# Time mixing of a decoder trunk: projections with features on partitions, plain float32 stationary weights, masks applied while a bank is emptied

## The chip, the core and the metric

The kernel runs on one core of one Trainium2 chip. The metric is the device time of the whole program in microseconds (us). A core has five instruction queues that matter here: TensorE (PE, with weight loads in a row of their own, PEld), VectorE (DVE), ScalarE (ACT), GpSimd (POOL) and SyncE (SP), which issues the transfers. Each engine executes its own instructions in order and waits for others on semaphores.

## The reference, cut to what matters

A two-layer decoder trunk with T = 256 tokens and D = 1024 features: a SwiGLU feed-forward, RWKV-7 time mixing, a second feed-forward, one shared K/V, and then a layer of feed-forward, windowed attention, feed-forward. All in float32. The part at issue is the time mixing of the first layer:

```python
xr, xw, xk, xv, xa, xg = [x + xx * mu[i] for i in range(6)]
r = xr @ w_rkv[0]
k = xk @ w_rkv[1]
v = xv @ w_rkv[2]
w = -jax.nn.softplus(-(w0 + jnp.tanh(xw @ w1) @ w2)) - 0.5
decay = jnp.exp(-jnp.exp(w.astype(f32)))
a = jax.nn.sigmoid(a0 + (xa @ a1) @ a2)
g = jax.nn.sigmoid(xg @ g1) @ g2
kk = heads(k * k_k)
kk = kk / jnp.maximum(jnp.linalg.norm(kk, axis=-1, keepdims=True), 1e-12)
k = k * (1.0 + (a - 1.0) * k_a)
b_h = kk * a_h
def step(S, inp):                        # over 256 tokens, 16 heads of 64
    sa = jnp.einsum('bhij,bhj->bhi', S, -kk_t)
    S = S * w_t + sa[..., None] * b_t + v_t[..., None] * k_t
    return S, jnp.einsum('bhij,bhj->bhi', S, r_t)
bonus = jnp.sum(r_h * k_h * r_k, axis=-1, keepdims=True) * v_h
return ((groupnorm(y) + bonus) * g) @ w_o
```

## The kernel before, in words

Weights of the feed-forwards, of keys, of receptance and of w_o are split into a high part (rounded to fp32r, on ACT, L145) and a low part (the difference, on DVE, L151, or in two halves on POOL, L149), and a product is three passes, high by high, high by low, low by high (mm3, L169, L173, L174). A list of numbers per stage (PK, PR, PWO and others) says which low parts POOL computes. Weights come in chunks of 512 KB through four buffers named wr, issued in order by SP.

The time mixing lies between the first and the second feed-forward. It uses the chunked form of the recurrence, with four chunks of 64 tokens. Tokens are in two halves of 128 (i = 0, 1). First come the shift difference xx and the mixes (L435). The low-rank projections of decay, rate and gate (tm_lora, L508, plain float32) and their second factors (L552) follow. Keys are projected per token half, tokens on partitions (tok_half), and so is the receptance for both halves (tok_both). With tokens on partitions, `keys` squares on ACT, sums per head on DVE (L562), raises to the power -1/2 on POOL (L564) and scales (L565); `decays` makes the running sum of the decay with a triangular matrix Lc (L576) and two exponentials (L581, L582), and takes 24 rows out of the result with 24 small transfers (L585); `elem` multiplies (L591 to L597, on POOL and DVE). Because the recurrence needs features on partitions, `flip` turns each of eight [128, 1024] tiles with eight PE transposes into two banks (L632) and copies the banks (L635) into the tiles AR (decayed receptance and minus the keys' direction) and BK (the other factors).

From AR and BK the diagonal blocks of 32x32 are formed (L663), copied out (L669) and inverted by a solver of 31 steps on DVE, two instructions per step (L696, L698). The values' projection (L498, plain float32, both halves) runs on PE beside the solver. Then come g_pass, three passes of 32 matmuls over 64 partitions (L721), whose banks ACT empties (L731, L784), masks on DVE (L729, eight of 128x1024), the product with the inverse (L813, L822), the two state steps (u_step L833, x_step L842), the biases and gates of the group norm (L770, L774, L780 to L782), the state S (L879, L882), the outputs (L863), the group norm (L909 to L922), and the projection with w_o.

The order of the instructions on each engine is made at build time by a scheduler that plays a timeline; the code's order is its input, and `mark` and `plan` add dependences for the splits. PSUM has six banks named bk and two named bt.

## Time and profile before

| what | before |
|---|---|
| time, median of 3 runs | 1136.38 us (1135.64 to 1136.39) |
| time of the profiled execution | 1136.9 us |
| span of its profile | 1135.1 us |
| granted TensorE clock, mean | 0.97 |
| PE busy | 1081.9 us, 95% |
| DVE busy | 667.5 us, 59% |
| ACT busy | 528.6 us, 47% |
| POOL busy | 153.4 us, 14% |

The time-mixing stage begins where PE ends the first feed-forward, shortly after 203 us, and the second feed-forward begins near 453 us. Outside this stretch PE is busy nearly throughout and at full clock. A number behind "x" is a count of instructions; PEclk is the granted TensorE clock, where 1.00 is full and 0.50 half; "<-" names what ended an engine's idle time. A float32 matmul stands in the profile as two records.

### The profile page before, as it was taken

To read this page: it belongs to the slowest core of one execution; us is meant where nothing else is said; L and a number is where in the kernel's file an instruction comes from. 1 tells how busy PE (TensorE), PEld (TensorE's weight loads), DVE (VectorE), ACT (ScalarE), POOL (GpSimd) and SP (SyncE) were. 2 spreads that over 40 slices of the span, in tenths; PEclk is the share of its full clock that TensorE was granted. 3 is DMA by queue.
4 is the path that set the end of the run, shared out by engine and by line. 5 is a ranking of instruction groups with operands and counts; after the bars stand their busy time and mean duration, and the time that the engine had idled before them with its cause. 6 is when DMAs were issued, how large, how long until landed. Compare 5 with 4: busy or idle time off the path is not lost.

```text
span 1135.1 us, 18594 instructions
## 1 busy us (share of the span) xinstructions
PE 1081.9 (95%) x7704; PEld 962.4 (85%) x7704; DVE 667.5 (59%) x843; ACT 528.6 (47%) x781; POOL 153.4 (14%) x113
## 2 busy tenths in 40 slices
...
GB/s 265 231 175 294 199 175 149 112 19 127 135 149 38 2 59 140 213 221 198 230 187 161 118 150 222 186 242 187 183 131 167 130 54 188 223 198 192 186 130 38
DMA packets 53651, 181.61 MB, mean 160 GB/s; under 512 B 9152, under 2 KB 9408, under 8 KB 53440
## 3 DMA queue, kind: packets, MB, share of 16 engines
...
q10 hardware_dynamic: 288, 0.52, 0.1%
q14 instruction: 23, 0.19, 0.1%
...
## 4 chain that ended last, share of the span: by engine, by line
PE 77%; DVE 7%; issue 5%; POOL 4%; ACT 3%; DMA 2%; SPq 1%; POOLq 0%; DVEq 0%; ACTq 0%
PE bk L173 22%; PE bk L174 22%; PE bk L169 22%; POOL W L149 4%; PE bk L498 2%; DVE W L151 1%; PE bk L721 1%; DVE xi L435 1%; ACT W L145 1%; PE bt L721 1%; DMA wr<-in_w_in_dram 1%; PE bk L1051 1%; SPq L585 1%; PE bk L833 1%; PE bt L250 1%
## 5 line engine op out<-in xcount | busy, mean ns | idle before, releaser
L151 DVE TENSOR_TENSOR W<-wr,W 128x1024 fp32r<-128x1024 f32 x274 | 347.0, 1273 | 296.2 <-ACT W L145 296.0
L145 ACT CAST W<-wr 128x1024 fp32r<-128x1024 f32 x308 | 320.3, 1048 | 396.0 <-PE bk L174 266.4
L169 PE MATMUL bk<-xth,W 128*128 128x256 f32 x1184 | 335.4, 283 | 0.0
L174 PE MATMUL bk<-xth,W 128*128 128x256 f32 x1184 | 334.8, 283 | 0.0
L173 PE MATMUL bk<-xtl,W 128*128 128x256 f32 x1184 | 334.7, 283 | 0.0
L173 PEld LDWEIGHTS bk<-xtl,W 128*128 128x128 f32 x1184 | 226.6, 191 | 1.3
L169 PEld LDWEIGHTS bk<-xth,W 128*128 128x128 f32 x1184 | 226.2, 191 | 1.3
L174 PEld LDWEIGHTS bk<-xth,W 128*128 128x128 f32 x1184 | 226.4, 191 | 0.0
L149 POOL TENSOR_TENSOR W<-wr,W 128x512 fp32r<-128x512 f32 x68 | 109.6, 1637 | 335.1 <-ACT W L145 331.9
L173 PE MATMUL bk<-W,g2k 128*128 128x512 f32 x352 | 137.8, 391 | 0.0
L169 PE MATMUL bk<-W,g2k 128*128 128x512 f32 x352 | 137.2, 391 | 0.0
L174 PE MATMUL bk<-W,g2k 128*128 128x512 f32 x352 | 136.7, 390 | 0.0
L183 POOL TENSOR_TENSOR rs<-rs,mhalf 128x1 f32<-128x1 f32 x24 | 13.2, 552 | 604.1 <-DVE rs L180 603.9
L169 PE MATMUL bk<-W,xth 128*128 128x256 f32 (+1 forms) x288 | 89.5, 315 | 3.9 <-ACT xth L255 3.9
L174 PE MATMUL bk<-W,xtl 128*128 128x256 f32 (+1 forms) x288 | 89.1, 313 | 1.7 <-DVE xtl L256 1.6
L173 PE MATMUL bk<-W,xth 128*128 128x256 f32 (+1 forms) x288 | 88.9, 312 | 0.6 <-DVE W L151 0.5
L174 PEld LDWEIGHTS bk<-W,g2k 128*128 128x128 f32 x352 | 66.1, 188 | 14.1
L169 PEld LDWEIGHTS bk<-W,g2k 128*128 128x128 f32 x352 | 66.2, 188 | 13.1
L173 PEld LDWEIGHTS bk<-W,g2k 128*128 128x128 f32 x352 | 66.3, 188 | 12.7
L169 PEld LDWEIGHTS bk<-W,xth 128*128 128x128 f32 x288 | 55.4, 193 | 7.6 <-ACT xth L255 4.7
L174 PEld LDWEIGHTS bk<-W,xtl 128*128 128x128 f32 x288 | 55.5, 194 | 5.2 <-DVE xtl L256 2.6
L173 PEld LDWEIGHTS bk<-W,xth 128*128 128x128 f32 x288 | 55.3, 193 | 4.1 <-DVE W L151 1.1
...
## 6 DMA issues: line engine op xcount, KB each, us to landing
wr<-in_w_in_dram SPq DMA_DIRECT2D x176, 512.0 KB, 4.0
...
```

Source lines behind the costliest of these rows:

```text
L145: self.follow(nc.scalar.copy(w[:, 0, :], raw), 0)
L149: self.follow(nc.gpsimd.tensor_tensor(w[:, 1, ns], raw[:, ns], w[:, 0, ns], op=ALU.subtract), 2)
L151: self.follow(nc.vector.tensor_tensor(w[:, 1, :], raw, w[:, 0, :], op=ALU.subtract), 1)
L169: m = mm(out, l[0], r[0], start=first, stop=False)
L173: mm(out, l[0], r[1], start=False, stop=False)
L174: return mm(out, l[1], r[0], start=False, stop=last)
L183: nc.gpsimd.tensor_tensor(t[:, 1:2], t[:, 0:1], self.mhalf, op=ALU.pow)
L250: t = self.nc.tensor.transpose(b[:, k * P:(k + 1) * P], xn[:, c:c + P], self.ident)
L435: eng.scalar_tensor_tensor(dst, self.xx[:, k, sl], self.cols[:, c:c + 1], self.uT[:, k, sl], op0=ALU.mult, op1=ALU.add)
L498: mm(accs[i][n], xf[:, k, sl], w[:, n * 512:n * 512 + 512], start=(k == 0), stop=(k == KT - 1))
L585: nc.sync.dma_start(DC[:, 2 * e or i, m:m + 1], Dt[i][64 * e + 63:64 * e + 64, m * P:(m + 1) * P])
L721: mm(b[:, x * P:(x + 1) * P], lhs(s, i, m), f(AR[s, 2 * m + i, 2 * e:2 * e + 2, :]), start=True, stop=True)
```

## The change

Keys and receptance are projected with features on partitions (feat_raw): the weights, in plain float32, are the stationary operand (128x128) and the mixed input with its 256 tokens moves. Per pair p of feature blocks, 16 matmuls fill one bank; two chunks of w_k or w_r, laid out anew on the host, serve one pair. The split of these weights and of xk and xr goes, and so do all flips. The running sum of the decay has the sigmoid as the stationary operand and a float32 triangle moving, so it too lands with features on partitions; its ends are one copy (DC) in place of the 24 transfers. The keys' norm takes a square on ACT with k_k as scale, a matmul with a two-column indicator HI, a maximum and a reciprocal on DVE, a square root on ACT that spreads the result over 64 columns, and four PE transposes per pair. The products are seven DVE instructions per pair; POOL computes none of them. The values' projection comes in two parts: the first token half at the start of the stage, the second behind the state steps of the first token half (u_step, x_step, u_step). Receptance takes the place beside the solver. The masks multiply while DVE empties the banks of g_pass. The diagonal blocks are copied by four ACT and four DVE instructions. The bonus sums are matmuls with HI. The lists PK, PR and PWO go, so the splits of w_o that POOL made are made on DVE. Pools wait per overlapping tile (`reuse_waits="tile"`).

```diff
...
-PWO = [(True, 0, 0), (False, -1, 2), (False, -3, 1), (False, -6, 1), (True, -2, 1), (False, -2, 7), (True, -2, 1), (True, -6, 7)]
...
-        self.pools[nm] = self.tc.alloc_tile_pool(name=f"{nm}{self.uid()}", bufs=bufs, side=side)
+        self.pools[nm] = self.tc.alloc_tile_pool(name=f"{nm}{self.uid()}", bufs=bufs, side=side, reuse_waits="tile")
...
+    def tok_raw(self, chunks, xf, i):
         mm = self.nc.tensor.matmul
-        accs = [[self.bank(), self.bank()] for _ in range(2)]
+        acc = [self.bank(), self.bank()]
+        sl = slice(i * P, (i + 1) * P)
         for k in range(KT):
             w = self.raw(chunks[k])
-            for i in range(2):
-                sl = slice(i * P, (i + 1) * P)
-                for n in range(2):
-                    mm(accs[i][n], xf[:, k, sl], w[:, n * 512:n * 512 + 512], start=(k == 0), stop=(k == KT - 1))
-        return accs
+            for n in range(2):
+                mm(acc[n], xf[:, k, sl], w[:, n * 512:n * 512 + 512], start=(k == 0), stop=(k == KT - 1))
+        return acc
+
+    def feat_raw(self, chunks, p, xf):
+        mm = self.nc.tensor.matmul
+        b = self.bank()
+        ws = [self.raw(chunks[2 * p + c]) for c in range(2)]
+        for j in range(2):
+            for k in range(KT):
+                c0 = (k % 4) * 256 + j * P
+                mm(b[:, j * T:(j + 1) * T], ws[k // 4][:, c0:c0 + P], xf[:, k, :], start=(k == 0), stop=(k == KT - 1))
+        return b
...
+        xv = self.tl("xt", [P, KT, T], tag="xth")
+        xk = self.tl("xt", [P, KT, T], tag="xtl")
+        self.mix(xv, 3, toks[0])
+        self.mix(xk, 2, toks[0])
+        self.tm_lora(0)
+        accv = [self.tok_raw(a["w_v"], xv, 0)]
+        self.mix(xk, 2, toks[1])
+        self.tm_lora(1)
...
+        Lc = self.cst[:, K_LC:K_LC + P]
+        for n in range(2):
+            for i in range(2):
+                b = self.bank()
                 for x in range(4):
-                    c0 = (mq * 4 + x) * P
-                    nc.tensor.transpose(b[:, x * P:(x + 1) * P], src[:, c0:c0 + P], self.ident)
-                o = cm(dst)[:, i, mq * 4:mq * 4 + 4, slots, :]
-                turn[0] += 1
-                (nc.scalar.copy if turn[0] % 4 else nc.vector.tensor_copy)(
-                    o, b.rearrange("p (m e t) -> p m e t", m=4, e=2))
+                    m = 4 * n + x
+                    mm(b[:, x * P:(x + 1) * P], sw[i][:, m * P:(m + 1) * P], Lc, start=True, stop=True)
+                v = b.rearrange("p (m e t) -> p m e t", m=4, e=2)
+                o = (slice(None), slice(4 * n, 4 * n + 4), slice(2 * i, 2 * i + 2))
+                nc.scalar.activation(Dp[o[0], o[1], o[2], 1:N + 1], v, AF.Exp, scale=-DEC)
+                nc.scalar.activation(Di[o], v, AF.Exp, scale=DEC)
...
+        for p in range(4):
+            qs = slice(4 * p, 4 * p + 4)
+            ms = slice(2 * p, 2 * p + 2)
+            kb = self.feat_raw(a["w_k"], p, xk)
+            kk, sq, am = (pk(t, [P, 2, T], 2) for t in ("kk", "sq", "am"))
+            for j in range(2):
+                nc.scalar.activation(sq[:, j], kb[:, j * T:(j + 1) * T], AF.Square, scale=col(C_KK, 2 * p + j))
+            for j in range(2):
+                nc.scalar.activation(kk[:, j], kb[:, j * T:(j + 1) * T], AF.Identity, scale=self.nkk[:, 2 * p + j:2 * p + j + 1])
+            bs = self.tbank()
+            for i in range(2):
+                for j in range(2):
+                    mm(bs[:, i * 4 + 2 * j:i * 4 + 2 * j + 2], sq[:, j, toks[i]], HI, start=True, stop=True)
+            rr = self.pp.tile([P, 2, 8], F32, name=f"rr{self.uid()}", tag="rr", bufs=2)
+            nc.vector.tensor_scalar(rr[:, 0, :], bs[:, 0:8], 1e-24, None, op0=ALU.max)
+            nc.vector.reciprocal(rr[:, 1, :], rr[:, 0, :])
+            rq = pk("rq", [P, 8, N], 2)
+            nc.scalar.activation(rq, rr[:, 1, :].unsqueeze(2).to_broadcast([P, 8, N]), AF.Sqrt)
+            rb = self.bank()
+            for j in range(2):
+                for i in range(2):
+                    h = i * 4 + 2 * j
+                    nc.tensor.transpose(rb[:, j * T + i * P:j * T + (i + 1) * P],
+                                        rq[:, h:h + 2, :].rearrange("p h t -> p (h t)"), self.ident)
+            for j in range(2):
+                nc.scalar.activation(am[:, j], av[p][:, j], AF.Identity, scale=col(C_KA, 2 * p + j),
+                                     bias=self.ka1[:, 2 * p + j:2 * p + j + 1])
+            di = Di[:, ms].rearrange("p m c t -> p (m c) t")
+            kmp = km[:, ms, :]
+            TT(kmp, kb.rearrange("p (j t) -> p j t", j=2), am, op=ALU.mult)
+            TT(BK[:, qs, 0:4:3, :], r4(c64(kmp)), r4(di), op=ALU.mult)
+            TT(kk, kk, rb.rearrange("p (j t) -> p j t", j=2), op=ALU.mult)
+            TT(AR[:, qs, 0:4:3, :], r4(c64(kk)), r4(dp(p))[:, :, :, 0:N], op=ALU.mult)
+            STT(kk, kk, -1.0, av[p], op0=ALU.mult, op1=ALU.mult)
+            TT(BK[:, qs, 1:3, :], r4(c64(kk)), r4(di), op=ALU.mult)
+            TT(BH[:, :, ms, :].rearrange("p i m x -> p m i x"),
+               BK[:, qs, 0:2, :].rearrange("p (m i) s t -> p m i (s t)", i=2),
+               Dp[:, ms, 0:4:2, N:N + 1].to_broadcast([P, 2, 2, P]), op=ALU.mult)
+        xr = self.tl("el", [P, KT, T], tag="xr")
+        self.mix(xr, 0, slice(0, T))
+        self.mix(xv, 3, toks[1])
+        nc.scalar.copy(DC, Dp[:, :, :, N])
...
+                v = bb[hh].rearrange("p (m b t) -> p m b t", m=KT, b=2)
+                o = Dg[:, hh * 16 + i:hh * 16 + 16:2, :]
+                nc.scalar.activation(o, v[:, :, 0, :], AF.Identity, scale=self.cst[:, K_BM:K_BM + 1])
+                STT(o, v[:, :, 1, :], self.cst[:, K_BM + 1:K_BM + 2], o, op0=ALU.mult, op1=ALU.add)
...
+        v0 = self.tl("el", [P, 2, 512], tag="v0")
+        for n in range(2):
+            nc.scalar.copy(v0[:, n, :], accv[0][n])
+
+        bo = self.tbank()
+        for p in range(4):
+            rp = self.feat_raw(a["w_r"], p, xr)
+            prod = self.tl("el", [P, 2, T], tag="pr")
+            TT(AR[:, 4 * p:4 * p + 4, 1:3, :], rp.rearrange("p (q e t) -> p q e t", e=2, t=N),
+               r4(dp(p))[:, :, :, 1:N + 1], op=ALU.mult)
+            for j in range(2):
+                STT(prod[:, j], rp[:, j * T:(j + 1) * T], col(C_RK, 2 * p + j), km[:, 2 * p + j, :],
+                    op0=ALU.mult, op1=ALU.mult)
+            for i in range(2):
+                for j in range(2):
+                    h = i * H + 4 * p + 2 * j
+                    mm(bo[:, h:h + 2], prod[:, j, toks[i]], HI, start=True, stop=True)
+        nc.scalar.copy(self.bon.rearrange("p i h -> p (i h)"), bo[:, 0:2 * H])
...
         def g_pass(lhs, dst, e, evac):
             for i in range(2):
-                for hh in range(2):
-                    s = slice(hh * 64, hh * 64 + 64)
-                    for mp in range(2):
-                        b = self.tbank() if mp else self.bank()
-                        for x in range(4):
-                            m = mp * 4 + x
-                            mm(b[:, x * P:(x + 1) * P], lhs(s, i, m), f(AR[s, 2 * m + i, 2 * e:2 * e + 2, :]),
+                for mp in range(2):
+                    bb = [self.bank(), self.tbank()]
+                    for x in range(4):
+                        m = mp * 4 + x
+                        for hh in range(2):
+                            s = slice(hh * 64, hh * 64 + 64)
+                            mm(bb[hh][:, x * P:(x + 1) * P], lhs(s, i, m), f(AR[s, 2 * m + i, 2 * e:2 * e + 2, :]),
                                start=True, stop=True)
-                        evac(cm(dst[hh])[:, i, mp * 4:mp * 4 + 4], b.rearrange("p (m s t) -> p m s t", m=4, s=2))
-
-        def mask(slot):
-            for t, k, e in ((GA, slot, 0), (GB, 1 - slot, 1)):
-                for hh in range(2):
-                    o = t[hh][:, :, k, :]
-                    TT(o, o, masks[:, e, k:k + 1, :].to_broadcast([P, 16, N]), op=ALU.mult)
-
-        low = lambda o, b: nc.scalar.copy(o[:, :, 0:2, :], b)
-        g_pass(lambda s, i, m: f(BK[s, 2 * m + i, 0:2, :]), GA, 0, low)
-        g_pass(lambda s, i, m: f(BK[s, 2 * m + i, 2:4, :]), GB, 1, low)
+                    for hh in range(2):
+                        evac(cm(dst[hh])[:, i, mp * 4:mp * 4 + 4],
+                             bb[hh].rearrange("p (m s t) -> p m s t", m=4, s=2))
+
+        def masked(e):
+            return lambda o, b: TT(o, b, masks[:, e].unsqueeze(1).to_broadcast([P, 4, 2, N]), op=ALU.mult)
+
+        g_pass(lambda s, i, m: f(BK[s, 2 * m + i, 0:2, :]), GA, 0, lambda o, b: masked(0)(o[:, :, 0:2, :], b))
+        g_pass(lambda s, i, m: f(BK[s, 2 * m + i, 2:4, :]), GB, 1, masked(1))
+        g_pass(lambda s, i, m: BH[s, i, m, :], GA, 1, lambda o, b: nc.scalar.copy(o[:, :, 2:4, :], b))
...
+        uv_in(0, [v0[:, n, :] for n in range(2)])
...
+        xv_in(0)
         u_step(0, 0)
         x_step(0)
+        u_step(0, 1)
+        uv_in(1, self.tok_raw(a["w_v"], xv, 1))
+        xv_in(1)
+        g2 = self.raw(a["lora2"][:, 2, :])
+        gng, gnb = self.gain(R_GNG), self.gain(R_GNB)
+        A0 = self.pp.tile([P, D], F32, name=f"gain{self.uid()}", tag="gain", bufs=3)
+        yy = self.tl("xt", [P, 2, H, N], tag="xth")
+        y = [yy[:, 0], yy[:, 1]]
+        B0 = y[1].rearrange("p h j -> p (h j)")
+        gn_bias(0, B0, B0)
+        gn_bias(1, gnb, y[0].rearrange("p h j -> p (h j)"))
         gn_gate(0, A0, B0)
-        u_step(0, 1)
         gn_gate(1, gng, gnb)
...
-    for j, nm in enumerate(("w_r", "w_k", "w_v")):
-        d[nm] = c(rkv[j].reshape(KT, P, D))
+    for j, nm in ((0, "w_r"), (1, "w_k")):
+        d[nm] = c(rkv[j].reshape(2, 4, P, 4, 256).transpose(3, 0, 2, 1, 4).reshape(KT, P, D))
+    d["w_v"] = c(rkv[2].reshape(KT, P, D))
...
```

On PE, in the projection of the keys, the rows before are these (W is a split weight chunk, xth and xtl the high and low parts of xk):

```order
L169 MATMUL bk_2145<-W_242_2030,xth_2079 128x512
L173 MATMUL bk_2145<-W_242_2030,xth_2079 128x512
L174 MATMUL bk_2145<-W_242_2030,xtl_2080 128x512
L169 MATMUL bk_2146<-W_242_2030,xth_2079 128x512
L173 MATMUL bk_2146<-W_242_2030,xth_2079 128x512
L174 MATMUL bk_2146<-W_242_2030,xtl_2080 128x512
```

and now, for the first pair and the beginning of the second (xtl is xk, sq the squares, rq the reciprocal norms):

```order
L487 MATMUL bk_2246<-xtl_2031,wr_2247 128x256 x4
L487 MATMUL bk_2246<-xtl_2031,wr_2249 128x256 x4
L487 MATMUL bk_2246<-xtl_2031,wr_2247 128x256 x4
L487 MATMUL bk_2246<-xtl_2031,wr_2249 128x256 x4
L582 MATMUL bt_2274<-cst,sq_2268 128x2 x4
L592 MATMUL bk_2284<-cst,rq_2282 128x128 x4
L487 MATMUL bk_2298<-xtl_2031,wr_2299 128x256 x4
```

The matmuls of the second pair stand behind the norm of the first: the indicator product L582 and the transposes L592.

On DVE, at the end of the solver (sw and kk are its tiles), the order before was

```order
L696 TENSOR_TENSOR kk_396_2913<-av_358_2766,sw_359_2767 128x31
L698 TENSOR_TENSOR sw_359_2767<-sw_359_2767,kk_396_2913 128x31
L151 TENSOR_TENSOR W_503_3821<-wr_3819,W_503_3821 128x1024
L736 STREAM_TRANSPOSE kk_432_3082<-sw_359_2767 128x32x32
L738 STREAM_TRANSPOSE av_433_3084<-sw_359_2767 128x32x32
L729 TENSOR_TENSOR GA_412_2982<-GA_412_2982,cst 128x16x64 x2
```

and is now (b, c and a are the solver's tiles, L683 is a mask out of a bank):

```order
L660 TENSOR_TENSOR c_2763<-a_2556,b_2557 128x112
L662 TENSOR_TENSOR b_2557<-b_2557,c_2763 128x4x28
L660 TENSOR_TENSOR c_2766<-a_2556,b_2557 128x87
L662 TENSOR_TENSOR b_2557<-b_2557,c_2766 128x3x29
L660 TENSOR_TENSOR c_2769<-a_2556,b_2557 128x60
L662 TENSOR_TENSOR b_2557<-b_2557,c_2769 128x2x30
L660 TENSOR_TENSOR c_2772<-a_2556,b_2557 128x31
L683 TENSOR_TENSOR GA_384_2776<-bt_2804,cst 128x4x128
L662 TENSOR_TENSOR b_2557<-b_2557,c_2772 128x31
L683 TENSOR_TENSOR xr_2777<-bk_2827,cst 128x4x128
L690 STREAM_TRANSPOSE c_2923<-b_2557 128x32x32
```

Of the sixteen L683, six more stand ahead of these rows among the solver's last steps, and eight behind.

On DVE, ahead of the state S (L882 before, L840 now), the order before was

```order
L782 TENSOR_TENSOR xth_3181<-xth_3181,bk_3454 128x512
L781 TENSOR_TENSOR gain_2979<-gain_2979,bk_3478 128x512
L782 TENSOR_TENSOR Di_410_2978<-Di_410_2978,bk_3478 128x512
L781 TENSOR_TENSOR gain_2979<-gain_2979,bk_3482 128x512
L782 TENSOR_TENSOR Di_410_2978<-Di_410_2978,bk_3482 128x512
L882 TENSOR_TENSOR kk_473_3486<-bk_3487,DC 128x512
```

and is now

```order
L745 TENSOR_TENSOR xth_3282<-BK_3099,bon 64x8x64 x4
L756 TENSOR_TENSOR gain_3281<-gain_3277,bk_3293 128x512
L148 TENSOR_TENSOR W_482_3621<-wr_3619,W_482_3621 128x1024
L745 TENSOR_TENSOR xth_3282<-BK_3099,bon 64x8x64 x2
L756 TENSOR_TENSOR gain_3281<-gain_3277,bk_3297 128x512
L745 TENSOR_TENSOR xth_3282<-BK_3099,bon 64x8x64 x2
L749 TENSOR_TENSOR xth_3282<-xth_3282,gain_3279 128x1024
L148 TENSOR_TENSOR W_484_3632<-wr_3630,W_484_3632 128x1024
L148 TENSOR_TENSOR W_486_3643<-wr_3641,W_486_3643 128x1024
L756 TENSOR_TENSOR gain_3277<-gain_3277,bk_3301 128x512
```

followed by another L756, an L749, two L757 and then L840. The biases (L745, before L770) write the tile xth, which holds the mixed input xv of the second half of the values' projection until that has run.

362 lines of the change are left out of this document (120 added, 242 removed).

## The prediction

> **What bounds the kernel now.** I read the page first: on which engine the span lies.
>
> ```profile
> span 1135.1 us, 18594 instructions
> PE 1081.9 (95%) x7704; PEld 962.4 (85%) x7704; DVE 667.5 (59%) x843; ACT 528.6 (47%) x781; POOL 153.4 (14%) x113
> PE 77%; DVE 7%; issue 5%; POOL 4%; ACT 3%; DMA 2%; SPq 1%; POOLq 0%; DVEq 0%; ACTq 0%
> ```
>
> TensorE bounds the program, but only the stretch from 203 to 453 us is changed. So the next view is the busy time of each engine by stage (busy in the order PE, PEld, DVE, ACT, POOL; then PEclk, DMA share, GB/s):
>
> ```profile
> 206.00:219.00 13.00, 8.53 (x68) 7.77 (x68) 12.82 (x19) 3.49 (x8) 11.78 (x10) 1.00 0.57 176
> 257.00:268.00 11.00, 6.26 (x24) 3.58 (x24) 8.83 (x20) 8.06 (x12) 4.06 (x2) 0.90 0.33 96
> 312.00:334.00 22.00, 22.00 (x61) 10.15 (x59) 20.19 (x50) 2.12 (x3) 2.43 (x2) 1.00 0.44 143
> 341.00:371.00 30.00, 30.00 (x194) 27.55 (x194) 16.50 (x18) 16.86 (x31) 0.00 (x0) 0.50 0.11 36
> 387.00:400.00 13.00, 13.00 (x101) 10.31 (x102) 4.07 (x7) 2.89 (x5) 0.00 (x0) 0.67 0.00 1
> 400.00:424.00 24.00, 20.97 (x488) 19.60 (x487) 17.14 (x32) 6.15 (x11) 0.00 (x0) 1.00 0.21 68
> ```
>
> Three limits follow each other. At 206 us DVE is full beside a full POOL. From 312 to 334 PE is full. From 341 to 371 PE is "100% busy" at half clock: 30 us that would be 15 at full clock. So a second question is when the clock falls. Cut into pieces of 3.41 us, at the phase at which the clock changes:
>
> ```profile
> 200.62:204.03 3.41, 3.22 (x14) 2.26 (x12) 1.51 (x3) 2.34 (x8) 1.64 (x2) 1.00 0.00 0
> 217.69:221.10 3.41, 1.20 (x4) 0.67 (x4) 3.41 (x7) 1.57 (x2) 2.46 (x2) 1.00 0.51 154
> 221.10:224.51 3.41, 2.76 (x7) 2.18 (x8) 3.12 (x5) 3.34 (x6) 0.00 (x0) 0.55 0.22 22
> 262.06:265.47 3.41, 0.52 (x2) 0.08 (x1) 3.41 (x11) 0.78 (x2) 0.00 (x0) 1.00 0.87 297
> 265.47:268.88 3.41, 1.89 (x9) 1.89 (x10) 3.41 (x8) 3.41 (x7) 2.84 (x1) 0.55 0.03 11
> 282.53:285.95 3.42, 1.60 (x12) 1.22 (x9) 3.42 (x2) 0.00 (x0) 3.42 (x3) 1.00 0.48 165
> 337.14:340.55 3.41, 2.08 (x25) 1.89 (x23) 2.29 (x6) 2.73 (x5) 0.00 (x0) 1.00 0.34 136
> 340.55:343.97 3.42, 3.42 (x25) 3.42 (x23) 3.42 (x3) 1.25 (x3) 0.00 (x0) 0.55 0.83 275
> ```
>
> A piece with 1.20 or 0.52 us of PE work is followed by a piece at half clock (0.55); one with 1.60 of full-size work (282.53) is not; one with 2.08 of 64-row work (337.14) is. Small tiles count for less, and then the clock stays low: the 30 us above.
>
> The chain of waits and the groups by line give the prices (start, duration; or duration, mean; for one line minimum, median and maximum):
>
> ```profile
> 260.52 0.60 SPq L585
> 301.45 0.72 PE bk L663 x18
> 308.75 9.44 PE bk L498 x22
> 355.86 2.00 PE bk L721 x8
> 375.56 2.96 PE bk L813 x93
> 381.70 3.04 PE bk L822 x61
> 386.98 3.39 PE bk L833 x30
> 390.37 3.60 PE bk L842 x32
> 403.12 3.40 PE bk L863 x82
> 420.55 3.78 PE bk L863 x92
> ```
>
> ```profile
> L240 DVE TENSOR_SCALAR t<-h,rs x4: 479/982/1498, 203.0 to 223.7; 128x512 f32<-128x512 f32 x4
> L205 DVE SCALAR_TENSOR_TENSOR h<-t,rs,h x6: 740/749/1757, 199.5 to 442.4; 128x512 f32<-128x512 f32 x6
> L696 DVE TENSOR_TENSOR kk<-av,sw x31: 191/374/1424, 311.7 to 337.5; 128x31 f32<-128x31 f32 x2, 128x60 f32<-128x60 f32 x2, 128x87 f32<-128x87 f32 x2, 128x112 f32<-128x112 f32 x2
> L698 DVE TENSOR_TENSOR sw<-sw,kk x31: 191/375/1286, 312.0 to 337.7; 128x31 f32<-128x31 f32 x2, 128x60 f32<-128x60 f32 x2, 128x87 f32<-128x87 f32 x2, 128x112 f32<-128x112 f32 x2
> L151 DVE TENSOR_TENSOR W<-wr,W x14: 1215/1225/3407, 221.6 to 448.5; 128x1024 fp32r<-128x1024 f32 x14
> L882 DVE TENSOR_TENSOR kk<-bk,DC x1: 691/691/691, 403.2 to 403.2; 128x512 f32<-128x512 f32 x1
> ```
>
> ```profile
> L770 DVE TENSOR_TENSOR xth<-BK,bon 64x512 f32<-64x512 f32 x8 | 5.2, 684 | 10.6 <-ACT BK L763 10.5
> L669 ACT COPY kk<-bk 32x256 f32<-32x256 f32 x8 | 2.9, 363 | 1.4 <-PE bk L663 1.3
> L731 ACT COPY GA<-bk 128x512 f32<-128x512 f32 x4 | 2.4, 592 | 0.0
> L512 ACT ACT_TABLE_LOAD x2 | 2.6, 1283 | 0.0
> L774 DVE TENSOR_TENSOR xth<-xth,Di 128x1024 f32<-128x1024 f32 x1 | 1.2, 1227 | 0.0
> L736 DVE STREAM_TRANSPOSE kk<-sw 128x1024 f32<-128x1024 f32 x1 | 2.1, 2111 | 0.0
> ```
>
> Prices from these rows. A float32 record of 512 columns takes 9.44/22 = 0.43 us, so one of 256 takes 0.215 and one of 128 0.107 (estimates by column count); each matmul is two records. A 64-row record with 128 columns is 2.00/8 = 0.25 at half clock, 0.125 at full; a 32x32 record 2.96/93 = 0.032 at full and 3.04/61 = 0.05 at half. A DVE instruction over 512 columns is 0.60 to 0.69, over 1024 1.23, and over 64 partitions 0.65; ACT takes 0.59 for 512 columns and 0.36 for 256.
>
> **The change part by part**, as a timeline after 203.84, where PE ends the feed-forward (200.62 + 3.22).
>
> *Start.* POOL's splits of w_k go, and with them ACT's casts. L240 is 479 ns at its fastest and 1498 at its slowest, L205 740 and 1757, the slow ones beside POOL: two of each cost 2 x 1.0 + 2 x 1.0 = 4 us. Bounds: 0, if the DVE is slow for another reason, and 6, if the small instructions at 211 to 216 us gain as well. I take 4.3: the first low-rank block ends at 212.6 in place of 216.9 (in the row 206 to 219 PE is busy for 8.53 of 13 us).
>
> *PE from there*, dense: first half of the values 32 x 0.43 = 13.75; eight transposes and 64 records of the second low-rank block, 72 x 0.107 = 7.7; second factors 8 x 0.43 + 16 x 0.215 = 6.9; running sum 32 x 0.107 = 3.4. Together 31.7: 244.3. The mixes and shifts of the second half run on DVE meanwhile (some 24 instructions of 0.35, 8.4 us, inside 13.75). If the values' chunks came late, that cover would be gone; four wr buffers are filled before.
>
> *Keys.* Four pairs at 32 x 0.215 = 6.9 are 27.5, against three passes before with the same PE time. But L582 and L592 stand ahead of the next pair's L487 on PE, and everything on PE queues behind them: ACT squares twice (0.72), the indicator matmuls (no row; at least 16 records at 0.032 = 0.5, at most three times that, I take 0.7), two small DVE instructions (0.3), ACT's root over 512 columns (0.59), four transposes (0.43), and five hand-overs at about 0.2. That is 3.8 per pair (bounds 2.8 and 4.8), three times 11.4, and 1.28 for one ACT table load, half of it hidden: 12.0. A gap of 3.8 fills one piece of 3.41 nearly always to less than 1.2 us, as at 217.69, so half clock follows: 1.2 us lost per gap, between 0 and 1.7, in all 3.6. End of keys: 287.4. Removed are the flips' PE work, the wait on ACT at 262 to 267 us (row 262.06: 0.52 busy), and the 24 transfers of 0.60 (the last at 260.52), which hold SP and so the loads of w_r behind them. Both gains are in the sum already, since it builds PE's work anew.
>
> *Last pair to solver.* 3.8 for the norm; seven DVE products at 0.65, 4.5; the second half of the blocks, 64 records at 0.72/18 = 0.04, 2.6; an ACT and a DVE copy, 1.3; the transposition, 2.1: 14.3. Start of the solver 301.7, with a little half clock 302.5 (bounds 300 and 305), against 311.7. That is 9.2 ahead.
>
> *Solver.* It took 26.2 (311.7 to 337.7 and its last 0.19). Without a copy that stood in it and POOL (2.43 us busy in that row) 23.3. It takes in the receptance's products for three pairs, 3 x 1.5 = 4.5, and seven masks, 4.6. End 334.9, against 337.9: 3.0 ahead. Receptance, 27.5 us of PE, lies beside it.
>
> *Masks and passes.* Behind the solver DVE has nine masks (5.4), two transpositions (4.2) and two small ones (0.9): 345.4. Eight masks of 1.23 and eight ACT copies go; but the copies' work is now on the engine of the solver. PE idles while the banks wait for DVE, much as at 337.14, so the clock is low when the rest comes: four runs of 8 records (8.0), 128 + 128 records of 32x32 (12.8), eight transposes (1.7), together 22.5 at half, 13.4 at full clock. I take half: 367.9.
>
> *First steps.* The values' product and three state steps: at half clock 3.4 (as u_step) + 3.4 + 3.6 + 3.4 = 13.8, at full some 7.8. I take 11, since part of the first overlaps the passes: 378.9.
>
> *Second half of the values.* 32 x 0.43 = 13.75, and 1.0 until the clock is back: 393.7. It stands on the path, where before it lay beside the solver. It frees the tile in which the biases are written, so DVE starts behind it: 8 x 0.65 + 2 x 1.23 + 6 x 0.60 + 3 splits at 1.22 (L151's least is 1215) = 14.9, with 0.6 for the first copy: L840 at 409.2. Before, L882 came at 403.2, and the same biases and gates ran under PE's 387 to 400 (DVE busy 4.07 of 13). The w_o splits in this block wait for their chunks only if these land later than that; the first buffers come free during the values.
>
> *Tail.* Three gate products between L840 and L841 and five w_o splits on DVE instead of POOL cost 1.4, DVE beside an idle POOL gains 1.0 at the end: 0.4.
>
> Sum: 409.2 - 403.2 + 0.4 = 6.4 at half clock throughout. With the waits at their lower bound (-3 on the keys, which pass on only in part, since the masks and passes then also move up) 3.4. I take +5: 1141.9 for the profiled execution, which lies 0.5 above the median shown, so 1141.4.
>
> **The rivals.** (1) *The clock holds.* If PE does not fall to half in the keys or behind the masks: 3.6 + 9.1 + 3.2 + 1.0 = 16.9 less than the half-clock sum, of which some 5 is lost again because DVE's masks then bound the start of the passes: 6.4 - 12 = -5.6, 1130.8. For it speaks the piece at 282.53, with 1.60 of work and no drop; against it 217.69 and 337.14. The Trainium skill, TensorE: Matmul & The Clock Gate, Part 1, has the clock fall after an idle window of about 3.4 us; by that rule a gap of 3.8 seldom holds a whole window, and the keys would stay at full clock. The row at 217.69, with 1.20 us of work in the piece ahead of a drop, speaks against reading the rule so strictly. (2) *Half of it*: the keys' gaps cost no clock, the passes do, and the steps run at 7.8: 6.4 - 3.6 - 3.2 = -0.4, 1136.0. (3) *A second drop in the tail.* DVE's 14.9 us ahead of L840 leave PE the products of the second half (1.7), gates (3.4), S (2.1) and the first outputs (3.4), some 10.6 of 15. If a piece falls under 2.08 of small work, the outputs and steps behind it run at half clock: 3.40 + 3.78 and two steps of 2.0 double, +8 to 11: +14, 1150.4. For it: at 337.14 just such work lost the clock. Against: from 400 to 424 PE is busy 20.97 of 24 and keeps 1.00. (4) *DVE was never slowed by POOL*: +4.3 on top, 1145.7.
>
> **How the numbers follow.** Chances: forecast 0.35, (1) 0.28, (2) 0.17, (3) 0.14, (4) 0.06. About 0.2%, 2.3 us, is what a measurement of this kernel tells from no change. Faster: (1) and a little of (2), 0.30. Within: most of (2) and the low edge of the forecast, 0.18. Slower: 0.52. The forecast's own range, with its waits at their bounds, is 1138 to 1146; the range for 8 in 10 reaches into (1) and (3): 1127 to 1151.
>
> **What would show it.** In the profile after: four runs of L487 in the keys with gaps of about 3.8 us ending on DVE or ACT, each followed by a piece with PEclk near 0.5; the solver's first L660 near 302 and its last L662 near 335; L676, L705 and L714 at PEclk 0.5 between 345 and 368; L477's second part near 379 to 394; L840 near 409, idle before L745 ended by PE or ACT, and no idle between L745 and L840. The forecast is wrong if L840 comes ahead of 403, and then the first of these marks that is early names the step.

## The result and the profile after

| | before | after |
|---|---|---|
| time, median | 1136.01 us (1133.69 to 1136.39, 4 runs) | 1162.51 us (1160.75 to 1163.79, 4 runs) |
| profiled execution, span | 1136.9 us, 1135.1 us | 1160.75 us, 1159.0 us |
| PE, DVE, ACT, POOL busy | 1081.9, 667.5, 528.6, 153.4 us | 1100.7, 626.5, 490.5, 85.1 us |

The ratio is 1.0237, with a 95% interval from 1.0217 to 1.0256: the change makes the kernel slower, by 26.5 us. The sign was forecast, with a chance of 0.52, but 1141.4 is far too little, and 1162.5 lies outside the range of 1127 to 1151. Executions of one program spread by up to 1.3% with the clock that they were granted (one kernel below took 1135.8 to 1139.7 us at a mean clock of 0.972 to 0.975 and 1146.0 to 1150.5 at 0.959 to 0.963), so a profile, which shows one execution, can lie some us off its kernel's median, and 2 or 3 us between two medians are not read as a difference.

On the page after, DVE, ACT and POOL all do less than before, and TensorE, which bounds the program, does more.

```profile
span 1159.0 us, 18676 instructions
PE 1100.7 (95%) x7816; PEld 984.0 (85%) x7816; DVE 626.5 (54%) x849; ACT 490.5 (42%) x732; POOL 85.1 (7%) x78
```

The busy times by stage, at two of the stretches shown of before and at four of the changed kernel's own (columns as there: PE, PEld, DVE, ACT, POOL, then PEclk, DMA share, GB/s):

```profile
206.00:219.00 13.00, 12.08 (x70) 8.78 (x70) 7.96 (x27) 3.48 (x8) 0.59 (x1) 1.00 0.31 92
312.00:334.00 22.00, 22.00 (x111) 19.59 (x110) 20.66 (x52) 0.00 (x0) 0.00 (x0) 1.00 0.46 144
336.50:353.00 16.50, 11.47 (x117) 10.65 (x116) 16.04 (x34) 1.52 (x3) 0.00 (x0) 0.87 0.11 37
353.00:386.97 33.97, 33.79 (x361) 31.85 (x363) 4.00 (x7) 12.38 (x22) 0.00 (x0) 0.50 0.00 1
396.48:410.43 13.95, 13.95 (x33) 6.01 (x34) 0.00 (x0) 1.40 (x3) 0.00 (x0) 1.00 0.66 218
410.45:425.00 14.55, 11.05 (x192) 7.96 (x194) 14.44 (x20) 5.69 (x8) 0.00 (x0) 0.96 0.66 224
```

From 206 to 219 us PE is now busy for 12.08 of 13 us, where it was busy for 8.53: the start went as forecast. The half clock behind the solver, 30 us before, is now 34 us (353.00 to 386.97). The values' second half (396.48) and the DVE block ahead of the state S (410.45) stand one behind the other, with the durations that were forecast for them. What was not forecast lies between 245 and 310 us, in the keys. Here each row is a pair of feature blocks (7.07, 9.27, 8.76, 9.29) or the gap behind it (6.36, 4.53, 4.91); the last row is receptance work ahead of the last block products:

```profile
245.49:252.56 7.07, 7.07 (x34) 5.89 (x32) 0.00 (x0) 3.63 (x9) 0.50 (x2) 1.00 0.10 20
252.56:258.92 6.36, 2.10 (x12) 1.95 (x13) 1.53 (x4) 4.58 (x8) 0.00 (x0) 0.81 0.40 143
258.92:268.19 9.27, 9.27 (x33) 7.46 (x32) 3.46 (x5) 0.00 (x0) 0.00 (x0) 0.76 0.09 16
268.19:272.72 4.53, 1.69 (x13) 1.54 (x13) 1.53 (x4) 3.18 (x7) 0.00 (x0) 1.00 0.56 203
272.72:281.48 8.76, 8.76 (x34) 7.07 (x32) 3.45 (x5) 0.00 (x0) 0.00 (x0) 0.81 0.07 17
281.48:286.39 4.91, 2.10 (x12) 1.95 (x13) 1.53 (x4) 2.20 (x5) 0.00 (x0) 0.74 0.53 183
286.39:295.68 9.29, 9.19 (x33) 7.38 (x32) 3.45 (x5) 0.00 (x0) 0.00 (x0) 0.77 0.08 20
302.79:309.76 6.97, 6.97 (x25) 5.47 (x26) 1.25 (x2) 0.00 (x0) 0.00 (x0) 0.64 0.01 2
```

A pair that follows a gap takes some 9 us in place of 7, at a clock of 0.76 to 0.81. What fills the first gap is told by the timeline (start, duration, engine, line, operation; in brackets the engine's idle time before and what ended it; weight loads are left out):

```profile
252.60 0.84 ACT L576 ACTIVATE sq<-bk,cols 128x256 f32<-128x256 f32 x2 [3.47 <-PE bk L487]
253.12 1.20 PE L582 MATMUL bt<-cst,sq 128*128 128x2 f32 x8 [0.56 <-ACT sq L576]
253.33 0.84 ACT L578 ACTIVATE kk<-bk,nkk 128x256 f32<-128x256 f32 x2
254.20 0.69 DVE L599 TENSOR_TENSOR km<-bk,am 128x512 f32<-128x512 f32 x1 [22.94 <-ACT kk L578]
254.81 0.16 DVE L584 TENSOR_SCALAR rr<-bt 128x8 f32<-128x8 f32 x1
254.93 0.69 DVE L600 TENSOR_TENSOR BK<-km,Di 128x512 f32<-128x512 f32 x1
254.93 1.09 ACT L595 ACTIVATE am<-av,ka,cols 128x256 f32<-128x256 f32 x2 [0.76 <-DVE km L599]
255.53 0.20 DVE L585 RECIPROCAL rr<-rr 128x8 f32<-128x8 f32 x1
256.04 1.28 ACT L587 ACT_TABLE_LOAD   x1
257.33 0.63 ACT L587 ACTIVATE rq<-rr 128x512 f32<-128x512 f32 x1
258.01 1.12 PE L592 MATMUL bk<-cst,rq 128*128 128x128 f32 x4 [3.70 <-ACT rq L587]
```

TensorE stands at L592 and waits for the root. Ahead of the root (L587), on the same two engines, stand four instructions that the norm does not need: ACT's scaling of the keys (L578); DVE's product of keys and rate (L599), which waits for L578 and stands ahead of the maximum (L584); DVE's product with the decay (L600), which stands ahead of the reciprocal (L585); and ACT's scaling for the pair after the next (L595), which waits for L599's tile. In the first pair the root also waits for a table load of 1.28 us.

**Where the 24 us of span come from.** In steps of 2 us, PE's time in the stage can be split into idle time, time lost to the clock (busy time times one minus PEclk) and work at full clock. From the end of the feed-forward (203.8 us before, 203.0 after) to the first projection of the second one (454.0 and 477.2) this gives

| | length | idle | lost to the clock | work at full clock |
|---|---|---|---|---|
| before | 250.2 | 22.6 | 28.3 | 199.2 |
| after | 274.2 | 28.4 | 31.8 | 214.0 |
| difference | +24.0 | +5.8 | +3.5 | +14.8 |

More than half is work. The keys' and receptance's products are most of it. These two rows of the timeline of before are the first of three passes and the first of the next three:

```profile
245.91 0.39 PE L169 MATMUL bk<-W,xth 128*128 128x512 f32 x1
246.60 0.39 PE L169 MATMUL bk<-W,xth 128*128 128x512 f32 x1
```

Three passes over 512 columns took 0.69 us, so the 64 of keys and receptance took 44 to 45 us; the plain float32 records that replace them take eight pairs of some 6.9 us (7.07 with the end of the last record), 55. That is some 11 us more. The indicator products L582 and L654, which did not exist, are some 8 us more, for 128 x 2 results: eight of them take 1.20 us, 0.15 each, about as long as the weight load beside them. The flips' transposes are gone (some 7 us less); the new transposes L592 (some 2 us) and a dearer running sum (3.7 us on L561, where L576 took 2.8) make up the rest.

### The profile page after: what moved, and what is told of

It reads as the page before. It is cut to its first block, busy times and chain, and to the rows that moved or that the text cites. A ratio compares the mean times of both kernels' runs of the same rounds, so it can differ in the third digit from the quotient of the medians.

```text
span 1159.0 us, 18676 instructions
## 1 busy us (share of the span) xinstructions
PE 1100.7 (95%) x7816; PEld 984.0 (85%) x7816; DVE 626.5 (54%) x849; ACT 490.5 (42%) x732; POOL 85.1 (7%) x78
## 3 DMA queue, kind: packets, MB, share of 16 engines
HBM read 181.98 MB, written 1.05 MB: 158 GB/s over the span
## 4 chain that ended last, share of the span: by engine, by line
PE 82%; DVE 7%; issue 4%; ACT 3%; POOL 3%; DMA 2%; SPq 0%; POOLq 0%; DVEq 0%; ACTq 0%
PE bk L170 21%; PE bk L171 21%; PE bk L166 21%; PE bk L487 6%; PE bk L477 2%; POOL W L146 2%; PE bk L497 1%; DMA wr<-in_w_in_dram 1%; PE bt L676 1%; PE bt L247 1%; DVE W L148 1%; ACT W L142 1%; DVE t L239 1%; PE bk L1008 1%; PE bk L780 1%
## 5 line engine op out<-in xcount | busy, mean ns | idle before, releaser
L148 DVE TENSOR_TENSOR W<-wr,W 128x1024 fp32r<-128x1024 f32 x270 | 335.5, 1249 | 289.8 <-ACT W L142 289.4
L142 ACT CAST W<-wr 128x1024 fp32r<-128x1024 f32 x292 | 303.6, 1048 | 366.1 <-PE bk L171 258.7
L146 POOL TENSOR_TENSOR W<-wr,W 128x512 fp32r<-128x512 f32 x44 | 69.7, 1610 | 211.4 <-ACT W L142 210.9
L166 PE MATMUL bk<-W,xth 128*128 128x256 f32 (+1 forms) x256 | 76.5, 302 | 1.0 <-ACT xth L252 0.9
L171 PE MATMUL bk<-W,xtl 128*128 128x256 f32 (+1 forms) x256 | 75.8, 300 | 0.9 <-DVE xtl L253 0.9
L170 PE MATMUL bk<-W,xth 128*128 128x256 f32 (+1 forms) x256 | 76.2, 301 | 0.3 <-DVE W L148 0.2
L166 PEld LDWEIGHTS bk<-W,xth 128*128 128x128 f32 x256 | 49.1, 193 | 3.0 <-ACT xth L252 1.6
L171 PEld LDWEIGHTS bk<-W,xtl 128*128 128x128 f32 x256 | 49.2, 193 | 2.6 <-DVE xtl L253 1.4
L170 PEld LDWEIGHTS bk<-W,xth 128*128 128x128 f32 x256 | 49.1, 193 | 2.1 <-DVE W L148 0.5
```

Source lines behind the costliest of these rows:

```text
L142: self.follow(nc.scalar.copy(w[:, 0, :], raw), 0)
L146: self.follow(nc.gpsimd.tensor_tensor(w[:, 1, ns], raw[:, ns], w[:, 0, ns], op=ALU.subtract), 2)
L148: self.follow(nc.vector.tensor_tensor(w[:, 1, :], raw, w[:, 0, :], op=ALU.subtract), 1)
L166: m = mm(out, l[0], r[0], start=first, stop=False)
L170: mm(out, l[0], r[1], start=False, stop=False)
L171: return mm(out, l[1], r[0], start=False, stop=last)
```

## The experiments

Two theories stood at the start. **A, the tail**: the values' second half and the biases behind it lie on the path between the first steps and S, 28.6 us from the second u_step's end to S where it was 4.5, and that is what is paid. **B, one chain from the keys on**: PE stands in the code's order behind each pair's norm, so that it idles, loses the clock, and ends receptance late; the passes, which need receptance, then run at half clock behind the solver rather than beside it.

All kernels compute everything that the reference asks for. The medians are device times; each ratio is against the kernel before on the same chip, with its 95% interval.

**The second half of the values at the start.** It goes to the start of the stage, and its result is copied to a free gain buffer.

```diff
+        self.mix(xv, 3, toks[1])
         accv = [self.tok_raw(a["w_v"], xv, 0)]
...
+        accv.append(self.tok_raw(a["w_v"], xv, 1))
...
-        uv_in(1, self.tok_raw(a["w_v"], xv, 1))
+        uv_in(1, [v1[:, n, :] for n in range(2)])
```

> The second token half of the values' projection runs at the start, right behind the first, and is copied out by ACT. Theory A (the loss lies between the last state step of the first token half and the state S, 28.6 us now against 4.5 before, because this projection and the DVE block of biases, gates and splits stand there one behind the other): the 13.95 us of PE move to a dense place, the solver starts about 14 us later (near 329.5), the stretch from that step to S falls to about 5 us, and the whole gains 24 - 14 = 10 us: near 1152. Theory B (the loss is the late start of the solver, by waits in the keys; the tail only shows it): the solver starts later still and the time does not fall: 1162 or above.

1163.03 us, ratio 1.0251 (1.0212 to 1.0290): no gain. The state still comes at 427.2 us (425.0 in the changed kernel). Everything ahead of it had moved back by the 14 us:

```profile
L664 DVE TENSOR_TENSOR c<-a,b x31: 192/357/426, 329.9 to 365.8; 128x31 f32<-128x31 f32 x2, 128x60 f32<-128x60 f32 x2, 128x87 f32<-128x87 f32 x2, 128x112 f32<-128x112 f32 x2
L844 DVE TENSOR_TENSOR c<-bk,DC x1: 684/684/684, 427.2 to 427.2; 128x512 f32<-128x512 f32 x1
```

The solver runs from 329.9 to 366 (315.6 to 346.9 in the changed kernel). PE has no free place at the start, and what is taken from one end is added at the other. Theory A falls in this form.

**The biases and gates behind S.** The ten lines from `g2 = ...` to `gn_gate(1, ...)` stand behind S in the code.

> The biases and gates of the group norm stand behind S in the code; in the order on DVE six instructions of the block (four gate products of the second operand, two of the first, and the second bias sum, 4.8 us) move behind the first product of S, while eight bias products, one sum and three splits stay ahead (10.1 us). Theory A (DVE's block sets when S comes): S comes 4.8 us earlier and the whole gains 3 to 5 us: 1157.5 to 1159.5. Theory B (S waits for PE, the block only fills DVE's wait): no change within 1 us.

1159.76 us, 1.0225 (1.0199 to 1.0251): 2.7 us less than the changed kernel by the medians, which these runs do not tell from nothing. S comes 6.2 earlier (418.8); the span of the profile (1155.1, the shortest of its four runs) is 3.9 shorter, so a part of the 6.2 is given back behind S.

**The next pair's products ahead of the norm.**

```diff
+        nxt = self.feat_raw(a["w_k"], 0, xk)
...
-            kb = self.feat_raw(a["w_k"], p, xk)
+            kb = nxt
+            if p < 3:
+                nxt = self.feat_raw(a["w_k"], p + 1, xk)
```

> The projection of the next pair of the keys is issued ahead of the norm of this pair, so PE has work while ACT and DVE make the norm. Theory A (the keys lose 16 us to three gaps of 4.7 to 6.5 us and 6 us to the half clock that follows each): the gaps fall to one or two of 4 us, keys and the blocks end 12 to 15 us earlier, the solver starts near 302, and since everything behind it stands in one chain the whole gains 12 to 15 us: 1148 to 1151. Rival (the gaps are slack, because receptance or the masks bound the end of the solver): the gain is below 4 us.

1143.17 us (10 runs), 1.0066 (1.0042 to 1.0089): 19.3 us less than the changed kernel, more than the 12 to 15 expected, from an edit of the order alone. The profile is of an execution of 1138.88 us. Split as above, its stage has some 15 us of idle time, 24 lost to the clock and 213 of work at full clock, where the changed kernel's has 28, 32 and 214.

```profile
L487 PE MATMUL bk<-xtl,wr x128: 379/379/635, 244.9 to 278.6; 128*128 128x256 f32 x128
L487 PE MATMUL bk<-xr,wr x128: 379/379/793, 285.9 to 319.2; 128*128 128x256 f32 x128
```

The keys end at 279 in place of 295.7 and receptance at 319.6 in place of 336.6, so most of the passes run beside the solver again, and S comes at 402.6, as before the change (403.2). Theory B is borne out: the idle time and the lost clock go, the work stays.

**Receptance behind the block products.** An ordering puts the first receptance product behind the last block product.

```diff
-            rp = self.feat_raw(a["w_r"], p, xr)
+            rp = self.feat_raw(a["w_r"], p, xr, lastb if p == 0 else None)
```

> The first matmul of receptance is held behind the last product of the diagonal blocks on PE, so 20 records of receptance (7.0 us at half clock) no longer stand ahead of the second part of the blocks. Theory A (the solver's start sets what follows): the solver starts 7 us earlier, near 308.6, and the whole gains 5 to 7 us: 1155.5 to 1157.5. Rival (receptance is the bound, since its last pair feeds the passes and its last products stand in the solver): its end moves little, and the gain is below 2 us.

1160.7 us (1154.01 to 1166.35), 1.0227 (1.0177 to 1.0277): 1.8 us less than the changed kernel by the medians, with an interval that holds theory A's 5 us as well as nothing. It did move the solver forward by 7.8 us, as it was to:

```profile
L662 DVE TENSOR_TENSOR c<-a,b x31: 193/359/426, 307.8 to 334.6; 128x31 f32<-128x31 f32 x2, 128x60 f32<-128x60 f32 x2, 128x87 f32<-128x87 f32 x2, 128x112 f32<-128x112 f32 x2
L487 PE MATMUL bk<-xr,wr x128: 379/379/793, 303.9 to 335.4; 128*128 128x256 f32 x128
```

Receptance ends at 335.8, nearly as it did (336.6), and the passes start there. But the profile is of the shortest run (1154.01 us), and in it S comes 8.6 us earlier (416.4) than in the changed kernel's, where the keys had ended only 1.6 earlier, so the rival is not shown by this kernel. With **both edits** the passes start at receptance's end too:

> Both earlier edits at once: the next pair of the keys ahead of the norm, and receptance held behind the block products. Theory A (one chain on PE, whose gaps and order set the end): the solver starts 5 to 7 us earlier than with the pipelined keys alone (299.6), near 293.5, and the whole is 3 to 6 us below it: 1137 to 1140. Rival (with the blocks held back, receptance ends later and the passes wait for it, as the small gain of the blocks alone hints): within 2 us of the pipelined keys, 1141 to 1145.

1146.63 us (10 runs), 1.0063 (1.0026 to 1.0100), no gain seen over the first of them alone: the solver starts at 293.6 and is done by 321, when receptance ends (322.0).

**The masks undone.** ACT empties the banks, and eight masks follow on DVE, as before the change.

> The changed kernel with the masks undone: ACT copies the banks of the passes, and eight masks of 128x1024 on DVE stand behind the solver. Theory M (masks on the solver's engine hold PE's banks; 39.8 us from the solver's end to the last product with the inverse): the solver ends 4.8 us earlier, PE has its passes behind it by then, and though 9.8 us of masks come, the last product with the inverse ends 4 to 7 us earlier; the whole gains as much: 1156 to 1159. Rival (the passes' and small products' time on PE at half clock is the bound, and the masks come back behind the solver): within 2 us of 1162.

1162.29 us, 1.0211 (1.0170 to 1.0252): no change. The solver ends 5 us earlier (341.8), the last product with the inverse only 2 (384.4), and S comes at 424.9, as it did (425.0).

**A block of ones.** A 128x128 matrix with a block of ones of 64x64 for each of its two heads is the stationary operand, and the squares move: the sums come out on all 64 features of a head, no root has to be spread and nothing transposed.

```diff
-            bs = self.tbank()
-            for i in range(2):
-                for j in range(2):
-                    mm(bs[:, i * 4 + 2 * j:i * 4 + 2 * j + 2], sq[:, j, toks[i]], HI, start=True, stop=True)
...
+            bs = self.bank()
+            mm(bs, self.cst[:, K_ON:K_ON + P], sq.rearrange("p j t -> p (j t)"), start=True, stop=True)
+            rq = pk("rq", [P, 512], 2)
+            nc.vector.tensor_scalar(rq, bs, 1e-24, None, op0=ALU.max)
+            nc.scalar.activation(rq, rq, AF.Sqrt)
+            nc.vector.reciprocal(rq, rq)
+            rb = rq
```

> The changed kernel with the keys' norm by a 128x128 block of ones as the stationary operand and the squares moving (512 columns, 0.86 us): the sums land on all partitions of a head, so the indicator products (1.2 us) and the four transposes (0.66 to 1.12) go, and PE waits in a pair for the squares alone; maximum, root and reciprocal run over 512 columns on DVE and ACT. Theory A (what costs is that PE stands behind the whole norm): the gaps fall from 4.7 to 6.5 us to about 1, no half clock follows, keys end 15 us earlier, and the whole gains 12 to 17 us: 1146 to 1151. Rival (the norm's time on DVE and ACT bounds each pair, with a reciprocal over 512 columns of unknown cost): pairs still come at intervals of 11 us or more, and the gain is below 4 us.

1131.72 us (10 runs), 0.9954 (0.9931 to 0.9976): 30.8 us less than the changed kernel, and faster than the kernel before. In the timeline PE waits only for the squares, and the next pair runs at full clock; split as above, the stage has some 15 us of idle time, 18 lost to the clock and 209 of work:

```profile
244.13 7.07 PE L487 MATMUL bk<-xtl,wr 128*128 128x256 f32 x32
252.13 1.12 PE L580 MATMUL bk<-sq,cst 128*128 128x512 f32 x2 [0.93 <-ACT sq L576]
253.09 7.07 PE L487 MATMUL bk<-xtl,wr 128*128 128x256 f32 x32
261.09 1.12 PE L580 MATMUL bk<-sq,cst 128*128 128x512 f32 x2 [0.93 <-ACT sq L576]
```

Receptance ends at 313.1, and three and a half of the four runs of the passes lie beside the solver (297.1 to 332.7):

```profile
L668 PE MATMUL bt<-AR,BK x64: 272/272/560, 313.1 to 329.5; 64*128 64x128 f32 x64
L668 PE MATMUL bk<-AR,BH x32: 272/272/373, 324.0 to 328.4; 64*128 64x128 f32 x32
L668 PE MATMUL bt<-AR,BH x32: 272/418/578, 329.8 to 337.1; 64*128 64x128 f32 x32
```

**The wait put back.** The block of ones removes a wait and lightens PE's work. To tell them apart, four transposes of the root per pair, whose result nobody reads, stand ahead of the next pair again.

```diff
+            un = self.tbank()
+            for x in range(4):
+                hold = nc.tensor.transpose(un[:, x * P:(x + 1) * P], rq[:, x * P:(x + 1) * P], self.ident)
...
-            kb = self.feat_raw(a["w_k"], p, xk)
+            kb = self.feat_raw(a["w_k"], p, xk, hold if p else None)
```

> The kernel with the squares moving against a 128x128 block of ones, with the wait put back and nothing else: four transposes of the spread root per pair, as many as the changed kernel has, whose result nobody reads, and the next pair's first key product ordered behind them. If it is the wait of TensorE on the norm that costs (the theory), the gaps of 4 to 6 us and the half clock in the pairs come back, solver start near 312 to 316, and the time goes from 1131.7 to 1150 to 1163. If it was the indicator products and transposes as work of TensorE (the rival), whose full-clock work was 5 us, four transposes per pair cost 1.7 us: 1132 to 1136.

1167.78 us (1167.70 to 1169.79), 1.0286 (1.0266 to 1.0306): all of the gain is gone, and more; it lies 5 us above the range expected.

```profile
259.70 1.11 PE L590 MATMUL bt<-cst,rq 128*128 128x128 f32 x4 [6.79 <-DVE rq L586]
260.61 8.08 PE L487 MATMUL bk<-xtl,wr 128*128 128x256 f32 x32
276.11 1.12 PE L590 MATMUL bt<-cst,rq 128*128 128x128 f32 x4 [5.36 <-DVE rq L586]
277.02 8.41 PE L487 MATMUL bk<-xtl,wr 128*128 128x256 f32 x32
```

It is the wait. It is longer here than in the changed kernel (6.8 and 5.4 us ahead of the transposes, where that had 3.7 and 2.3), since the reciprocal over 512 columns lies in it. Split as above, the stage has some 36 us of idle time, 35 lost to the clock and 211 of work, against 15, 18 and 209 with the ones alone: nearly all of the loss is idle time and clock. The keys end 24.0 us later than with the ones alone and the program 36.1 later, 1.5 us for each (the two medians come from two chips, whose kernels before differ by 1.1). In the pair of kernels that differ in order alone it was 19.3 us for 16.6 us of earlier keys, 1.2 for each. The changed kernel's keys end 17.4 later than with the ones; at 1.2 to 1.5 that is 20 to 26 of its 30.8 us, an estimate, and 5 to 11 are left for the lighter work.

**Biases and gates behind S, once the keys are free.** The block of ones and the second edit above together.

> The kernel with the block of ones, and the biases and gates put behind the state S in the code. The state came at 393.7 us with the block of ones; without the block of biases and gates ahead of it, it should come some 6 us earlier, as it did in the changed kernel (425.0 to 418.8). If the bonus and gates are then hidden beside the outputs: 1127 to 1130. If they return in the group norm's tail, as half of it did in the changed kernel: 1130 to 1133.

1124.39 us (1122.73 to 1127.91), 0.9906 (0.9877 to 0.9934): below the range expected and the best kernel of this study, 10.9 us under the one before on its chip (1135.29 us). S comes at 386.8 in place of 393.7, and the program is 5 to 7 us shorter (5.5 by the spans, 7.3 by the medians, which come from two chips). In the changed kernel the same edit moved S by 6.2 and gave 3.9 by the spans and 2.7 by the medians; whether it is worth more once the keys are free, these few runs do not show.

**What did not add up.** The other edits were also put on top of the block of ones: the order of pairs, blocks and masks,

> Pipelined keys, block of ones, receptance behind the blocks, masks behind the solver. Theory A (the loss against the kernel before is idle PE and half clock in the keys, plus 15 us of added PE work, of which the block of ones takes back 3): solver starts near 290, the whole lies 4 to 8 us below the pipelined keys: 1135 to 1139, level with the kernel before. If the masks help as well: 1128 to 1134. Rival (the passes and steps at half clock take back what comes earlier): 1140 to 1145.

1134.58 us, 0.9980 (0.9956 to 1.0003), none of them worth anything now; the early second half of the values,

> Block of ones for the norm, and both halves of the values' projection at the start. Theory A (everything behind the keys is one chain on PE; moving the second half only moves 13.95 us of PE along it): within 3 us of the block of ones alone (1131.7). Theory B (in the block-of-ones kernel the second half in the tail waits 5.4 us for its own weights and 3.2 us more for w_o, and DVE's block of 14.6 us stands behind it; these go, and the steps that would then lose the clock are fewer): 8 to 15 us below it, 1117 to 1124.

1136.34 us, 1.0005 (0.9982 to 1.0029), 4.6 above the ones alone, where neither theory had it. In the profile, of an execution of 1141.92 us, the solver (311.0 to 358.6) took in masks and the splits of w_o and became 12 us longer than with the ones alone. The bias row of the norm, which waits for one of three gain buffers, was given a tile of its own in the changed kernel,

> The changed kernel with the bias row of the group norm in a tile of the solver instead of one of the three gain buffers. Theory: in the changed kernel SP waits from 432.6 to 451.8 us for a gain buffer, and the last chunk of w_o (issued at 453.39, split at 459.69) stands behind that wait, and DVE's last instructions of the second half's norm stand behind the split; with the buffer free the chunk is loaded in time and the end comes 4 to 7 us earlier: 1155 to 1158. Rival (the norm's own chain on DVE sets the end, the split only fills a wait; DVE is idle there for 1.6 us alone): below 2 us.

1167.09 us, 1.0269 (1.0249 to 1.0290), no gain. The wait went and the norm of the second half ended 6.3 us earlier, but PE's clock fell in the tail, from 0.87 to 0.66 between 425 and 447 us and from 1.00 to 0.90 between 447 and 500. The changed kernel first, then this one:

```profile
425.00:447.00 22.00, 19.09 (x373) 18.17 (x370) 14.88 (x30) 4.99 (x10) 0.00 (x0) 0.87 0.07 27
```

```profile
425.00:447.00 22.00, 21.20 (x344) 20.22 (x341) 13.64 (x27) 4.99 (x10) 0.00 (x0) 0.66 0.09 26
```

Why it fell there was not tried. The last two put that tile, and then the order of pairs too, on the kernel with ones and early values:

> The same with the bias row out of the gain buffers. If the last chunk of w_o waits for a gain buffer in that kernel too: 4 to 6 us below the block of ones with both halves at the start; if not, within 2 us of it.

> The same with the next pair of the keys issued ahead of the norm. The block of ones leaves gaps of 0.9 us and 1.1 us of matmul in each pair, three times; theory A: pipelining takes back the three gaps of 0.9 and no clock, 2 to 3 us; rival: the order of the block products behind it changes and nothing is gained, within 2 us.

1137.81 us, 1.0021 (0.9996 to 1.0045), and 1143.29 us, 1.0079 (1.0054 to 1.0104): neither gains, and the second is slower than the first by more than the noise.

## Why the prediction was right in sign and wrong in size

The timeline of the prediction can be laid beside the changed kernel's, step by step. The profiled execution took 18.9 us more than the 1141.9 forecast for it. Three steps failed, and they make up 18.7 us: the keys' gaps and the half clock behind them, the way from the last pair to the solver, and the passes behind the solver. All three took TensorE to be ready earlier than it was. The sign, forecast with 0.52, owes something to luck: the +5 behind it is far smaller than the error of its steps.

| step of the prediction | forecast | measured | miss |
|---|---|---|---|
| start and dense PE work, to the first key product | 244.3 | 245.5 | +1.2 |
| keys, length | 43.1 | 50.2 | +7.1 |
| last pair to solver | 15.1 | 19.9 | +4.8 |
| solver, length | 32.4 | 31.3 | -1.1 |
| solver's end to last product with the inverse | 33.0 | 39.8 | +6.8 |
| first steps | 11.0 | 9.7 | -1.3 |
| second half of the values | 14.75 | 13.95 | -0.8 |
| DVE block ahead of L840 | 15.5 | 14.6 | -0.9 |
| tail, and 5 taken for a sum of 6.4 | 0.4, -1.4 | 2.1, 0 | +3.1 |

**Right.** The start: the first low-rank block ended at 213.4 (forecast 212.6), and L202, the old L205, took 750 ns each where two of four took over 1.0 us beside POOL; rival 4 falls. The solver's length, though the mix of what it took in differs, the second half of the values and the DVE block, all within 1.3 us. Rivals 1 and 2 fall: PE did lose the clock in the keys and in the passes. Of rival 3 there is a small part: from 425 to 447 the clock was 0.87, and from 447 on 1.00, while DVE's block ahead of S passed at 0.96.

**Keys: the gap and what follows it were too short.** The step put "3.8 per pair" and half of a table load, 12.0 us in all; the gaps were 6.36, 4.53 and 4.91, 15.8 in all. Its sum followed the chain of the norm from instruction to instruction, but left out the four instructions (L578, L599, L600, L595) that stand between its links on the same engines in program order; the row of L599 waiting for L578, and that of L595 waiting for L599, show them. The half clock behind a gap cost 2.0 us per pair (9.1 in place of 7.07), not 1.2. Cut at the phase at which the clock changes, the pieces ahead of the three drops are these:

```profile
253.12:256.53 3.41, 1.20 (x8) 1.04 (x8) 1.53 (x4) 2.63 (x6) 0.00 (x0) 1.00 0.58 202
270.19:273.61 3.42, 1.39 (x9) 1.29 (x10) 1.86 (x5) 1.61 (x3) 0.00 (x0) 1.00 0.31 114
280.43:283.85 3.42, 2.25 (x13) 1.61 (x11) 0.67 (x2) 1.57 (x4) 0.00 (x0) 1.00 0.74 231
282.10 1.20 PE L582 MATMUL bt<-cst,sq 128*128 128x2 f32 x8 [0.62 <-ACT sq L576]
```

They hold 1.20, 1.39 and 2.25 us of PE work, where the step expected less than 1.2 nearly always. In the third piece PE never stood still for more than 0.62 us, and 1.20 of its 2.25 us were two-column records (the last row). The half clock then lasted for two pieces behind the first and the third gap (256.53 to 263.36 and 283.85 to 290.68), where the step's upper bound of 1.7 us had only one. By the Trainium skill, TensorE: Matmul & The Clock Gate, Part 1, the clock falls after an idle window of about 3.4 us; these pieces do not agree with an idle window taken strictly, as 217.69 of before did not.

**Last pair to solver: PE's queue again.** The step listed the products, the blocks, the copies and the transposition, and let receptance lie "beside" the solver. But 20 records of receptance stood on PE ahead of the last block products, and ran at a clock of 0.64. The chain of waits of the changed kernel:

```profile
300.45 2.34 PE bk L627 x48
302.79 6.97 PE bk L487 x20
310.39 8.40 PE bk L487 x38
```

The blocks that the solver waits for ran at 309.7 to 310.2, between these two runs of L487. Taking the 20 records away did start the solver 7.8 us earlier, but the medians do not tell its gain from nothing, while its shortest run had S 8.6 us earlier. So this step was wrong in its time, and how much of its miss reached the end stays open.

**Passes behind the solver: too few.** The step counted "four runs of 8 records" of L676 there, 32 records. Receptance, which they need, ended at 336.6, 10 us before the solver; when the solver ended, some 105 of 192 records had not begun, and 84 ran from 353 us on, at half clock:

```profile
353.18 1.44 PE L676 MATMUL bt<-AR,BK 64*128 64x128 f32 x5 [3.61 <-DVE GA L683]
L676 PE MATMUL bk<-AR,BH x32: 325/417/578, 348.6 to 363.0; 64*128 64x128 f32 x32
L676 PE MATMUL bt<-AR,BH x32: 417/417/578, 360.1 to 371.2; 64*128 64x128 f32 x32
```

From the solver's end the step put 10.5 us of DVE work and then 22.5 of PE; measured were 6.3 until PE went on and 33.5 behind. The prediction took the order on DVE from the program and did not ask when the operands of the passes would be there. Its own prices speak against 32 records: 27.5 us of receptance beside a solver of 32.4 leave 4.9 us for the other 160, which at 0.125 each take 20. In the passes PE also stood still for 5.2 us, 3.61 of them in the first row, until a mask (L683) had emptied a bank. The clock had fallen before that, at 348.7, behind a piece with 2.17 us of such 64-row work, much as at 337.14 of before (2.08). And with the masks undone S came no earlier, as far as one execution shows, so the wait for the masks does not seem to decide the time by itself.

In each of the three misses PE comes late. The kernel with the next pair's products ahead of the norm took back 19.3 us and that with the ones 30.8, more than the misses of 18.9, since the forecast too had gaps in the keys.

**A price that was wrong by itself.** The keys' pairs were said to be "27.5, against three passes before with the same PE time". The 27.5 was right (four times some 6.9 at full clock), but three passes took 0.69 per product, 22 us. No number of the timeline hung on it, since PE's work was built anew. The indicator products were counted as at least 16 records per pair; there are 8, but at 0.15 us rather than at most 0.1, so they took 1.20 us where the step took 0.7. With both prices right, the reader of the prediction would have seen that TensorE, the bound, gets over 10 us more work.
